# A hybrid encoder layer on one core: the wide input projection from fp32r pairs to scaled fp16 pairs, in two weight passes

## The chip, the core and the metric

The kernel runs on one NeuronCore of a Trainium2 chip. Its engines work through queues of their own: TensorE (PE in the profile, its weight loads PEld), VectorE (DVE), ScalarE (ACT), GpSimd (POOL) and SyncE (SP), whose queue here only issues DMAs. The metric is the device time of one execution in microseconds (us). Of the kernel before there are three timed runs, 911.38, 912.72 and 910.8 us, median 911.38.

## The reference

One layer of a hybrid encoder, 2048 tokens and 16 meta tokens in front of them, width 1024. Tokens are normalised (RMSNorm), and one projection feeds two mixers:

```python
u = rmsnorm(h, norm_g) @ w_in
pool_in, pool_gate, c_q, c_kv, k_r, attn_gate = jnp.split(u, SPLIT_POINTS, axis=-1)   # 512,512,256,128,64,512
pool_out = silu(pool_gate) * pool_mixer(pool_in, pool_w, pool_scale)   # trailing means over 2,4,8,16 tokens
...                                              # low-rank attention, 4 heads, chunks of 64 tokens
attn_out = silu(attn_gate) * attn
h + concat([pool_out, attn_out]) @ w_out         # then a last RMSNorm
```

The change concerns the three parts of the projection that are 512 wide: the pooling input, its gate and the attention gate, 1536 columns together.

## The kernel before

**Split numbers.** To come near fp32, a product is made of three matmuls of pairs: each operand is split into a rounded high part and the remainder, and high*high, low*high and high*low are summed. Scores and projections hold the parts as fp32r. The weighted sum over the values (`pv`, line 470, tiles `o`) has its parts in fp16.

**Stages.** A first stage makes the queries, keys and values of all tokens and starts the attention of the short chunks. The attention follows, chunk by chunk in the order of `ORDER`: chunks 20 to 31 in groups of four, then 19 down to 8. For a chunk `scores` runs twice (two pairs of heads): PE computes score blocks (lines 407 to 411), DVE takes the maximum (line 413), ACT the exponential (line 434), the fp16 pair is made on ACT and on POOL or DVE (lines 437 and 439), and a DMA transpose on SP's queue (line 446) turns it for `pv`. Up to chunk 17 `pv` comes one chunk after its scores, later right behind them.

**The wide projection** is the work of `run_pass` (lines 658 ff.). Its 1536 columns are 12 weight blocks `m` of 128: 0 to 3 the pooling input, 4 to 7 its gate, 8 to 11 the attention gate. The tokens are eight sub-ranges `i`: the first has 272 (16 of them meta), the others 256. `mproj` computes one block on one sub-range as 24 matmuls, 8 slices of the depth by three products. `PASSES = ((0,), (1, 2, 3), (4, 5, 6, 7))` gives three passes over the weights. Within a pass blocks go in pairs (`MORDER`: 0 and 4, 1 and 5, ...), and each pair runs over the pass's sub-ranges. Pass 0 is spread over the attention of the chunks 13 to 8 (`FILL`); passes 1 and 2 follow the attention.

**What is loaded.** `load_w` fetches a block (512 KB) and splits it in four pieces on ACT and on POOL or DVE, once in each pass: 36 times. `load_x` fetches a sub-range in two halves, multiplies by the norm's gain and splits it on ACT and DVE. The token's own factor (`rbc`, one over its root mean square) is applied to the result, line 588 (`u`) and line 611 (`gt`). Sub-range 0 is loaded at chunk 15, sub-ranges 1 to 3 when the attention is over (its memory is used), 4 to 7 in the last pair of pass 1.

**Behind a block**: `pool_in` makes window sums on DVE and splits the result, `gate` makes the SiLU from a tanh, `pool_out` multiplies by the pooling weights (three matmuls, line 620). At the end the output projection (line 800) takes 16 tiles of tokens. Before a tile its operand is split (lines 787 to 790) into the buffers that the weight blocks used.

**Order.** A scheduler puts each engine's instructions in order by times that it simulates. On the chip each engine works through its list in that order, and so does SP with its DMAs.

## Time and profile before

| | us |
|---|---|
| median of three timed runs (910.8 to 912.72) | 911.38 |
| the profiled execution | 913.35 |
| its span, first to last instruction | 911.5 |
| PE busy | 875.0 (96%) |
| DVE, ACT, POOL busy | 569.7, 442.7, 357.4 |
| matmuls of the wide projection, line 579 | 2304 |

The span is what the profiler saw of one execution. A PE matmul's record is longer than the time until the next can start, so that busy time says less than the distance from start to start. PEclk and "granted clock" are the share of TensorE's full clock: 1.0 is 2.4 GHz, 0.5 is 1.2 GHz.

### The profile page before, as it was taken

The page shows a single profiled execution, that of the slowest core. Times are in us where ns is not written, and L with a number is a line of the kernel's source. Part 1 is how long each engine was busy: PE and PEld are TensorE (multiplying, and loading weights), DVE is VectorE, ACT ScalarE, POOL GpSimd, SP SyncE. Part 2 cuts the span into 40 slices and gives each one's busy share as a digit, 9 for nine tenths or more (in the row PEclk, how much of TensorE's full clock was granted, in tenths as well). Part 3 has the DMA queues.
Part 4 walks back from the last instruction along what each step waited for, and adds up shares of the span by engine and source line. Part 5 has one row for each costly group of instructions (what it writes and reads, how often), then busy time and mean ns, then how long its engine had stood idle before and what let it go on. Part 6 is the DMA issues. An engine that isn't in the chain of part 4 may idle for free.

```text
span 911.5 us, 16442 instructions
## 1 busy us (share of the span) xinstructions
PE 875.0 (96%) x5799; PEld 794.2 (87%) x5799; DVE 569.7 (63%) x1309; ACT 442.7 (49%) x1217; POOL 357.4 (39%) x572
## 2 busy tenths in 40 slices
PE   9799899999999999899969999999999999999996
...
PEclk9899999999999999999979999999999999999999
...
GB/s 266 207 175 178 143 48 104 173 142 126 157 154 135 125 161 134 210 177 167 150 209 198 47 93 70 200 90 47 38 34 25 139 93 93 93 92 93 105 81 46
DMA packets 210413, 114.39 MB, mean 125 GB/s; under 512 B 169641, under 2 KB 196747, under 8 KB 210331
## 3 DMA queue, kind: packets, MB, share of 16 engines
...
q8 instruction: 45, 0.74, 0.3%
...
## 4 chain that ended last, share of the span: by engine, by line
PE 69%; DMA 10%; DVE 8%; ACT 6%; issue 4%; POOL 2%; ACTq 0%; SPq 0%; POOLq 0%; DVEq 0%
PE mp L579 26%; PE op L800 20%; PE o L470 6%; PE tok L221 4%; DVE st L413 2%; DMA yr<-hT_in 2%; DMA raw<-hT_in 2%; PE qa L310 2%; ACT p L434 2%; PE s L407 2%; PE s L409 2%; PE s L408 2%; PE s L411 2%; PE s L410 2%; DMA pt<-hl 1%
## 5 line engine op out<-in xcount | busy, mean ns | idle before, releaser
L579 PE MATMUL mp<-y,wh 128*128 128x256 f32 (+1 forms) x1536 | 285.1, 284 | 4.5 <-DVE y L548 2.8
L579 PEld LDWEIGHTS mp<-y,wh 128*128 128x128 f32 x1536 | 242.1, 191 | 5.0 <-DVE y L548 3.0
L579 PE MATMUL mp<-y,wl 128*128 128x256 f32 (+1 forms) x768 | 217.8, 284 | 0.0
L800 PE MATMUL op<-wo,mh 128*128 128x512 f32 (+1 forms) x528 | 160.4, 386 | 0.0
L579 PEld LDWEIGHTS mp<-y,wl 128*128 128x128 f32 x768 | 146.2, 190 | 0.1
L439 POOL TENSOR_TENSOR hl<-p,hl 128x512 f16<-128x512 f32 (+4 forms) x104 | 102.8, 1010 | 98.1 <-ACT hl L437 92.8
L434 ACT ACTIVATE p<-s,st 128x512 f32<-128x512 f32 (+8 forms) x168 | 99.3, 601 | 63.7 <-DVE st L419 51.3
L800 PEld LDWEIGHTS op<-wo,mh 128*128 128x128 f32 x528 | 98.0, 188 | 22.2
L800 PE MATMUL op<-wo,ml 128*128 128x512 f32 (+1 forms) x264 | 102.3, 388 | 0.0
L470 PE MATMUL o<-pt,vh 128*128 128x256 f16 x544 | 92.8, 274 | 6.5 <-DMA pt<-hl 6.2
L413 DVE TENSOR_REDUCE st<-s 128x1 f32<-128x512 f32 (+6 forms) x154 | 88.6, 588 | 15.0 <-PE s L411 14.0
L567 POOL TENSOR_TENSOR wl<-wr,wh 128x256 fp32r<-128x256 f32 x96 | 80.3, 858 | 31.9 <-ACT wh L565 29.5
L437 ACT CAST hl<-p 128x512 f16<-128x512 f32 (+6 forms) x168 | 82.0, 540 | 4.8 <-DMA pt<-hl 4.3
L802 DVE TENSOR_TENSOR xr<-op,xr 128x512 f32<-128x512 f32 (+1 forms) x33 | 22.3, 676 | 92.9 <-PE op L800 92.9
L470 PE MATMUL o<-pt,vl 128*128 128x256 f16 x272 | 74.5, 274 | 0.0
L804 ACT ACTIVATE osq<-xr 128x512 f32<-128x512 f32 (+1 forms) x33 | 20.4, 617 | 97.7 <-DVE xr L802 88.2
L470 PEld LDWEIGHTS <-vh 128*128 128x128 f16 x544 | 51.3, 98 | 17.6 <-issue 5.8
L565 ACT CAST wh<-wr 128x256 fp32r<-128x256 f32 x144 | 47.8, 403 | 31.3 <-PE mp L579 18.1
L789 POOL TENSOR_TENSOR ml<-mix,mh 128x512 fp32r<-128x512 f32 x16 | 21.7, 1355 | 102.0 <-ACT mh L787 102.0
L800 PEld LDWEIGHTS op<-wo,ml 128*128 128x128 f32 x264 | 49.6, 188 | 10.5
L589 POOL COPY carry<-u 128x16 f32<-128x16 f32 x32 | 15.8, 494 | 88.6 <-DVE u L588 88.6
L439 DVE TENSOR_TENSOR hl<-p,hl 128x512 f16<-128x512 f32 (+7 forms) x64 | 42.4, 663 | 12.5 <-ACT hl L437 12.3
...
## 6 DMA issues: line engine op xcount, KB each, us to landing
wr<-w_m_in SPq DMA_DIRECT2D x36, 512.0 KB, 3.7
xt<-hcat_in SPq DMA_DIRECT2D x16, 512.0 KB, 5.0
xr<-hcat_in SPq DMA_DIRECT2D x16, 512.0 KB, 3.7
raw<-hT_in SPq DMA_DIRECT2D x15, 512.0 KB, 6.4
out_dram<-xr SPq DMA_DIRECT2D x15, 512.0 KB, 2.6
yr<-hT_in SPq DMA_DIRECT2D x14, 512.0 KB, 3.8
...
wor<-w_out_in SPq DMA_DIRECT2D x8, 512.0 KB, 4.1
```

The costliest lines, as they stand in the source:

```text
L221: nc.tensor.matmul(ps[:T, :448], lhsT=a[:, k, :T], rhs=w[:, k], start=k + i == 0, stop=k == KT - 1 and i == 2)
L413: nc.vector.reduce_max(out=mx[:, bi:bi + 1], in_=ps[:, :w], axis=AX.X)
L434: nc.scalar.activation(out=pr[:, o:o + w], in_=pss[bi][:, :w], func=AF.Exp, bias=nb_, accum_out=sm[:, bi:bi + 1] if nb > 1 else tot)
L437: nc.scalar.copy(out=hl[:, 0, sl], in_=pr[:, sl])
L439: eng.tensor_tensor(out=hl[:, 1, sl], in0=pr[:, sl], in1=hl[:, 0, sl], op=ALU.subtract)
L470: nc.tensor.matmul(ps[:, :2 * P], lhsT=v, rhs=x, start=i == 0, stop=i == len(ops) - 1)
L565: nc.scalar.copy(out=wh[:, sl], in_=wr[:, sl])
L567: eng.tensor_tensor(out=wl[:, sl], in0=wr[:, sl], in1=f(wh[:, sl]), op=ALU.subtract)
L579: nc.tensor.matmul(ps[:, :n - sk], lhsT=a[:, k], rhs=x[:, k, sk:n], start=e == 0, stop=e == 3 * KT - 1)
L789: nc.gpsimd.tensor_tensor(out=ml[:, 0:4], in0=m, in1=f(mh[:, 0:4]), op=ALU.subtract)
L800: nc.tensor.matmul(ps[:, :w], lhsT=x[:, k], rhs=y[:, sl], start=i == 0, stop=i == 3 * KT - 1)
L802: nc.vector.tensor_add(out=xr[:, sl], in0=ps[:, :w], in1=xr[:, sl])
```

## The change

The two operands of the wide projection become fp16 pairs: high and low parts in fp16 instead of fp32r, three products as before.

- fp16 has a smaller range, so both are multiplied by powers of two first. For the tokens it comes from the largest gain (`gmx`, once, behind the first stage). For a weight block it comes from the block's largest entry: each of the 12 blocks is fetched once more during the attention of the chunks 20 to 31 (`SCAN`, tile `ws`), DVE takes the largest absolute value, and behind the last one `weight_scales` spreads the maxima over the partitions with 12 small fp32 matmuls (one more for `gmx`).
- The token's factor moves into `load_x`: DVE multiplies each slice by gain and `rbc` in place, ACT rounds to fp16, POOL subtracts, in pieces of two slices. The factors at lines 588 and 611 go; what undoes the scales is applied by ACT (`winv`, `whalf`) or within `psi`.
- fp16 tokens need half the memory: `PASSES = ((0, 1), (2, 3, 4, 5, 6, 7))`, 24 block loads for 36. Pass 0 has twice the work in the same places of the attention. Sub-ranges 0 and 1 are loaded at the chunks 17 and 16, 2 and 3 during pass 0, 4 to 7 in the first pair of pass 1.
- `load_w` splits in two pieces of 512: one on ACT and DVE, the other on ACT (twice) and POOL. The output projection's split operands get buffers of their own.

```diff
+WPIECE = 512
+XSC = 9
+WSC = 14
...
+SCAN = {23 - m if m < 4 else 31 - m if m < 8 else 39 - m: m for m in range(12)}
...
+def spread_max(nc, ps, cols, n, ident, out):
+    for i in range(n):
+        nc.tensor.matmul(ps[:, i * P:(i + 1) * P], lhsT=cols[:, i:i + 1].broadcast_to([P, P]), rhs=ident, start=True, stop=True)
+    nc.vector.reduce_max(out=out, in_=ps[:, :n * P].rearrange("p (n q) -> p n q", n=n), axis=AX.X)
...
-    PASSES = ((0,), (1, 2, 3), (4, 5, 6, 7))
+    PASSES = ((0, 1), (2, 3, 4, 5, 6, 7))
...
         for k0 in (0, 4):
-            raw = wtile("wr", 4 * n, F32, f"yr{i}_{k0}", XPOOL.get(i)).rearrange("p (k t) -> p k t", k=4)
+            raw = wtile("wr", 4 * n, F32, f"yr{i}_{k0}").rearrange("p (k t) -> p k t", k=4)
             nc.sync.dma_start(out=raw, in_=hT[:, k0:k0 + 4, o:o + n])
             for k in range(k0, k0 + 4):
-                nc.scalar.mul(out=xh[:, k], in_=raw[:, k - k0], mul=gin_t[:, k:k + 1])
-                nc.vector.scalar_tensor_tensor(out=xl[:, k], in0=raw[:, k - k0], scalar=gin_t[:, k:k + 1], in1=f(xh[:, k]),
-                                               op0=ALU.mult, op1=ALU.subtract)
+                nc.vector.scalar_tensor_tensor(out=raw[:, k - k0], in0=raw[:, k - k0], scalar=gxs[:, k:k + 1], in1=rbc,
+                                               op0=ALU.mult, op1=ALU.mult)
+            for k in (k0, k0 + 2):
+                nc.scalar.copy(out=xh[:, k:k + 2], in_=raw[:, k - k0:k - k0 + 2])
+                nc.gpsimd.tensor_tensor(out=xl[:, k:k + 2], in0=raw[:, k - k0:k - k0 + 2], in1=xh[:, k:k + 2], op=ALU.subtract)
...
+            sc = wsc[:, m:m + 1]
+            for n, o in enumerate(range(0, D, WPIECE)):
+                sl = slice(o, o + WPIECE)
+                if n % 2 == 0:
+                    nc.scalar.mul(out=wh[:, sl], in_=wr[:, sl], mul=sc)
+                    nc.vector.scalar_tensor_tensor(out=wl[:, sl], in0=wr[:, sl], scalar=sc, in1=wh[:, sl], op0=ALU.mult, op1=ALU.subtract)
+                else:
+                    nc.scalar.mul(out=wr[:, sl], in_=wr[:, sl], mul=sc)
+                    nc.scalar.copy(out=wh[:, sl], in_=wr[:, sl])
+                    nc.gpsimd.tensor_tensor(out=wl[:, sl], in0=wr[:, sl], in1=wh[:, sl], op=ALU.subtract)
+            wts[(ps_, m)] = (wh.rearrange("p (k c) -> p k c", k=KT), wl.rearrange("p (k c) -> p k c", k=KT))
...
-        nc.vector.tensor_tensor(out=u[:, 16:16 + n], in0=ps[:, :n], in1=rbcs[i], op=ALU.mult)
+        nc.scalar.mul(out=u[:, 16:16 + n], in_=ps[:, :n], mul=winv[:, g:g + 1])
...
-        nc.vector.tensor_tensor(out=gt, in0=ps[:, :G], in1=rbcs[i][:, n - G:n], op=ALU.mult)
-        nc.scalar.activation(out=th, in_=gt, func=AF.Tanh, scale=0.5)
-        nc.vector.scalar_tensor_tensor(out=gt, in0=th, scalar=1.0, in1=gt, op0=ALU.add, op1=ALU.mult)
+        nc.scalar.activation(out=th, in_=ps[:, :G], func=AF.Tanh, scale=whalf[:, m:m + 1])
+        if m < 8:
+            nc.vector.scalar_tensor_tensor(out=gt, in0=th, scalar=1.0, in1=ps[:, :G], op0=ALU.add, op1=ALU.mult)
+        else:
...
+                if ps_ == 0 and pi == 2 * XPRE[n]:
+                    load_x(2 + n)
+                if ps_ == 0 and pi == len(MORDER) - 2 and n == 0:
+                    load_w(1, *MORDER[0:2])
+                if ps_ == 1:
+                    if pi == 0 and n < 4:
...
+        if c in SCAN:
+            m = SCAN[c]
+            ws = att2.tile([P, D], F32, name=f"ws{m}", tag="ws", bufs=2)
+            with tc.issue_after(last_tr[0]):
+                nc.sync.dma_start(out=ws, in_=w_m[m])
+            nc.vector.tensor_reduce(out=wmx[:, m:m + 1], in_=ws, axis=AX.X, op=ALU.max, apply_absolute_value=True)
+            if m == 11:
+                weight_scales()
...
+        if c == X1_AT:
+            load_x(1)
+        if c == W0_AT:
+            load_w(0, *MORDER[0:2])
...
-        mh = wtile("wh", D, F32R, f"mh{t}").rearrange("p (k t) -> p k t", k=KT)
-        ml = wtile("wl", D, F32R, f"ml{t}").rearrange("p (k t) -> p k t", k=KT)
+        mh = c2.tile([P, D], F32R, name=f"mh{t}", tag="mh", bufs=2).rearrange("p (k t) -> p k t", k=KT)
+        ml = c2.tile([P, D], F32R, name=f"ml{t}", tag="ml", bufs=2).rearrange("p (k t) -> p k t", k=KT)
```

What moved, by the order of the instructions (a name holds its block or chunk, then a buffer number: `pt23_0` is the first transposed page of chunk 23, `mp1_4` block 4 on sub-range 1, `yr4_0` the raw tokens of sub-range 4, `x2` the fp16 tokens of the sub-ranges 4 and 5).

SP's queue at the change from chunk 7 to chunk 23, before:

```order
L446 DMA_TRANSPOSE pt7_1_1944<-hl7_0_1_1937 128x5x128
L446 DMA_TRANSPOSE pt7_0_1934<-hl7_1_0_1965 128x4x128
L446 DMA_TRANSPOSE pt7_1_1944<-hl7_1_1_1971 128x5x128
L446 DMA_TRANSPOSE pt23_0_2064<-hl23_0_0_2060 128x8x128
L446 DMA_TRANSPOSE pt23_1_2071<-hl23_0_1_2067 128x8x128
```

And in the change:

```order
L472 DMA_TRANSPOSE pt7_1_1961<-hl7_0_1_1954 128x5x128
L472 DMA_TRANSPOSE pt7_0_1951<-hl7_1_0_1982 128x4x128
L472 DMA_TRANSPOSE pt7_1_1961<-hl7_1_1_1988 128x5x128
L798 DMA ws0_2044<-w_m_in 128x1024
L472 DMA_TRANSPOSE pt23_0_2084<-hl23_0_0_2080 128x8x128
L472 DMA_TRANSPOSE pt23_1_2091<-hl23_0_1_2087 128x8x128
```

The fetch of a block's scan now stands between the transposes of two chunks, and so it does for twelve chunks.

PE's queue behind the last attention product (`av2`), before:

```order
L494 MATMUL av2_1_6293<-ol2_5800,wvh_121 128x256
L494 MATMUL av2_1_6293<-oh2_5799,wvh_121 128x256
L494 MATMUL av2_1_6293<-oh2_5799,wvl_122 128x256
L494 MATMUL av2_1_6293<-ol2_5800,wvh_121 128x256
L579 MATMUL mp1_0_6427<-y1_6404,wh1_0_6365 128x256
L579 MATMUL mp1_0_6427<-y1_6404,wl1_0_6366 128x256
L579 MATMUL mp1_4_6464<-y1_6404,wh1_4_6377 128x256
L579 MATMUL mp1_4_6464<-y1_6404,wl1_4_6378 128x256
```

In the change, the same place and the place where the sub-ranges 4 and 5 (`x2`) are first used:

```order
L520 MATMUL av2_1_6756<-oh2_6136,wvl_129 128x256
L520 MATMUL av2_1_6756<-ol2_6137,wvh_128 128x256
L611 LDWEIGHTS wh1_4_6837
L611 MATMUL mp2_4_6961<-x1_5644,wh1_4_6837 128x256
L611 LDWEIGHTS wh1_0_6830
```

```order
L611 MATMUL mp3_4_7050<-x1_5644,wh1_4_6837 128x256
L654 MATMUL pm2_0_7079<-plh2_0_6957,pwh_4835 128x256
L654 MATMUL pm2_0_7079<-plh2_0_6957,pwl_4836 128x256
L654 MATMUL pm2_0_7079<-pll2_0_6958,pwh_4835 128x256
L611 LDWEIGHTS wh1_0_6830
L611 MATMUL mp4_0_7106<-x2_6990,wh1_0_6830 128x256
L611 LDWEIGHTS wl1_0_6831
L611 MATMUL mp4_0_7106<-x2_6990,wl1_0_6831 128x256
```

Before, PE meets a sub-range that is fetched after the attention (`y1`) at once. Now 99 matmuls of `mp1_11`, `mp2_0`, `mp2_4`, `mp3_0` and `mp3_4` stand between the last `o` matmul and the first on `x2`; the fp16 matmuls have weight loads of their own.

POOL's queue there, before:

```order
L684 TENSOR_TENSOR at0_1536<-at0_1536,gt0_10_6326 128x256
L567 TENSOR_TENSOR wl1_4_6378<-wr1_4_6375,wh1_4_6377 128x256
L684 TENSOR_TENSOR at0_1536<-at0_1536,gt0_11_6356 128x256
L567 TENSOR_TENSOR wl1_4_6378<-wr1_4_6375,wh1_4_6377 128x256
L567 TENSOR_TENSOR wl1_1_6520<-wr1_1_6517,wh1_1_6519 128x256
L589 COPY carry_5082<-u1_0_6452 128x16
L567 TENSOR_TENSOR wl1_1_6520<-wr1_1_6517,wh1_1_6519 128x256
L587 COPY u2_0_6566<-carry_5082 128x16
```

In the change:

```order
L621 COPY carry_4806<-u2_0_6949 128x16
L619 COPY u3_0_7038<-carry_4806 128x16
L725 TENSOR_TENSOR at1_2021<-at1_2021,gt1_11_6899 128x256
L578 TENSOR_TENSOR x2_6990<-yr4_4_7003,x2_6990 128x512 x2
L844 TENSOR_TENSOR ml0_9663<-mix0_4808,mh0_9662 128x512
L844 TENSOR_TENSOR ml1_9733<-mix0_4808,mh1_9732 128x512
L578 TENSOR_TENSOR x2_6990<-yr5_0_7086,x2_6990 128x512 x2
L621 COPY carry_4806<-u3_0_7038 128x16
L578 TENSOR_TENSOR x2_6990<-yr4_0_6993,x2_6990 128x512 x2
L578 TENSOR_TENSOR x2_6990<-yr5_4_7096,x2_6990 128x512
L619 COPY u4_0_7131<-carry_4806 128x16
L578 TENSOR_TENSOR x2_6990<-yr5_4_7096,x2_6990 128x512
```

The subtractions of the tokens are now POOL's, and two of the output projection's operands (`ml0`, `ml1`) have come forward between them. Before they stand behind the whole of the wide projection.

## Rows read from the trace of the kernel before

**Rows 1.** The page's slices: busy tenths in 40 slices, granted clock.

```profile
PE   9799899999999999899969999999999999999996
...
PEclk9899999999999999999979999999999999999999
```

**Rows 2.** Busy time by stretch; columns in the second line.

```profile
core 0: us, PE busy (x) PEld busy (x) DVE busy (x) ACT busy (x) POOL busy (x), PEclk, DMA share, GB/s
180.00:360.00 180.00, 178.82 (x1226) 157.86 (x1225) 117.46 (x288) 123.12 (x352) 82.29 (x108) 1.00 0.84 142
360.00:440.00 80.00, 76.54 (x569) 71.18 (x567) 65.89 (x155) 53.42 (x157) 43.89 (x69) 1.00 0.79 182
440.00:460.00 20.00, 16.50 (x136) 15.71 (x134) 15.64 (x44) 13.47 (x46) 12.14 (x19) 1.00 0.57 138
460.00:480.00 20.00, 13.89 (x84) 12.38 (x85) 8.72 (x20) 7.61 (x20) 2.57 (x4) 0.74 0.83 241
480.00:490.00 10.00, 9.18 (x74) 8.80 (x74) 10.00 (x25) 7.84 (x22) 5.89 (x8) 1.00 0.60 183
490.00:720.00 230.00, 230.00 (x1922) 230.00 (x1921) 158.63 (x346) 75.38 (x197) 85.51 (x131) 1.00 0.26 80
```

**Rows 3.** The chain that ended last, in order of time: start us, us, what.

```profile
41.59 3.75 PE we L284 x16
...
301.86 5.25 PE o L470 x48
...
463.01 7.31 DMA yr<-hT_in
...
686.08 40.24 PE mp L579 x336
726.32 178.09 PE op L800 x792
```

**Rows 4.** Line 579: duration ns min/median/max, first and last start us, forms.

```profile
L579 PE MATMUL mp<-y,wh x1536: 274/283/582, 383.2 to 726.0; 128*128 128x256 f32 x184, 128*128 128x272 f32 x8
...
L579 PE MATMUL mp<-y,wl x768: 274/283/415, 383.4 to 725.9; 128*128 128x256 f32 x184, 128*128 128x272 f32 x8
```

**Rows 5.** PE in time, the instructions after idle time: start, us, what [idle <-releaser].

```profile
460.49 0.38 PE L470 MATMUL o<-pt,vh 128*128 128x256 f16 x2 [2.44 <-DMA pt<-hl]
...
468.25 0.39 PE L579 MATMUL mp<-y,wh 128*128 128x256 f32 x1 [1.70 <-ACT y L547]
...
471.81 0.80 PE L579 MATMUL mp<-y,wh 128*128 128x256 f32 x2 [2.83 <-DVE y L548]
```

**Rows 6.** Groups on POOL by form: xcount | busy us, mean ns | idle before.

```profile
L439 POOL TENSOR_TENSOR hl<-p,hl 128x512 f16<-128x512 f32 x36 | 45.3, 1261 | 69.6 <-ACT hl L437 67.9 <-issue 1.1 <-DVE ql L314 0.5
...
L789 POOL TENSOR_TENSOR ml<-mix,mh 128x512 fp32r<-128x512 f32 x16 | 21.7, 1355 | 102.0 <-ACT mh L787 102.0
L589 POOL COPY carry<-u 128x16 f32<-128x16 f32 x32 | 15.8, 494 | 88.6 <-DVE u L588 88.6
...
L587 POOL COPY u<-carry 128x16 f32<-128x16 f32 x32 | 11.2, 351 | 8.4 <-DVE pl L599 6.2 <-issue 1.1
```

**Rows 7.** A group on DVE by form.

```profile
L653 DVE TENSOR_TENSOR wo<-wor,wo 128x1024 fp32r<-128x1024 f32 x8 | 9.6, 1246 | 1.9 <-ACT wo L652 1.8
```

**Rows 8.** DVE in time, from 483 us.

```profile
484.30 1.66 DVE L548 SCALAR_TENSOR_TENSOR y<-yr,gains_t,y 128x256 fp32r<-128x256 f32 x4
...
486.55 0.41 DVE L604 TENSOR_TENSOR pll<-pl,plh 128x256 fp32r<-128x256 f32 x1
...
487.91 0.41 DVE L599 SCALAR_TENSOR_TENSOR pl<-w,u 128x256 f32<-128x256 f32 x1
```

**Rows 9.** POOL in time, from 483 us.

```profile
486.43 1.95 POOL L589 COPY carry<-u 128x16 f32<-128x16 f32 x1 [2.66 <-DVE u L588]
```

**Rows 10.** DMA issues: xcount, KB each, median us from issue to landing.

```profile
wr<-w_m_in SPq DMA_DIRECT2D x36, 512.0 KB, 3.7
...
pt<-hl SPq DMA_TRANSPOSE x168, 3.2
```

More of the change, by code (lines that the diff above doesn't have):

```diff
@@ L11 @@
 F16 = mybir.dt.float16
+I32 = mybir.dt.int32
 AF = mybir.ActivationFunctionType
@@ L50 @@
 WRB = 2
-XPOOL = {1: 0, 2: 1, 3: 0}
 TBB = 2
@@ L121, in hymba @@
     nc.gpsimd.memset(rall, 1.0)
+    gxs = cp.tile([P, KT], F32, name="gxs")
+    ginv = cp.tile([P, 1], F32, name="ginv")
+    wsc = cp.tile([P, 12], F32, name="wsc")
+    winv = cp.tile([P, 12], F32, name="winv")
+    whalf = cp.tile([P, 12], F32, name="whalf")
+    psi = cp.tile([P, H], F32, name="psi")
+    wmx = cp.tile([P, 12], F32, name="wmx")
     ca_cm, cap = open_pool("ca", side="left")
@@ L345, in hymba @@
     pts = {}
+    last_tr = [None]
     rsum = {}
@@ L542, in load_x @@
-        xl = l_[:, :KT * n].rearrange("p (k t) -> p k t", k=KT)
+        if i // 2 not in xpairs:
+            xpairs[i // 2] = big((1, 0, 2, 3)[i // 2], f"x{i // 2}", F16, 2 * KT * (SUBS[i][1] + SUBS[i + 1][1]))
+        at = 0 if i % 2 == 0 else 2 * KT * SUBS[i - 1][1]
+        xp = xpairs[i // 2][:, at:at + 2 * KT * n].rearrange("p (a k t) -> p a k t", a=2, k=KT)
+        xh, xl = xp[:, 0], xp[:, 1]
+        rbc = cw["pool"].tile([P, n], F32, name=f"rbc{i}", tag="rbc", bufs=2, padded_shape=[P, 272])
@@ L620, in pool_out, with weight_scales @@
             nc.tensor.matmul(ps[:, :G], lhsT=w[:, g], rhs=x, start=e == 0, stop=e == 2)
-        nc.vector.scalar_tensor_tensor(out=mixg[i][:, g], in0=ps[:, :G], scalar=psh_t[:, g:g + 1],
+        nc.vector.scalar_tensor_tensor(out=mixg[i][:, g], in0=ps[:, :G], scalar=psi[:, g:g + 1],
                                        in1=gt, op0=ALU.mult, op1=ALU.mult)
     cw = {}
+    def weight_scales():
+        for m in range(0, 12, 4):
+            spread_max(nc, bank("m", f"wmx{m}"), wmx[:, m:m + 4], 4, ident, wsc[:, m:m + 4])
+        power_scale(nc, wsc, winv, wsc, WSC)
+        nc.vector.tensor_scalar(out=winv, in0=winv, scalar1=ginv, scalar2=float(2.0 ** -WSC), op0=ALU.mult, op1=ALU.mult)
+        nc.vector.tensor_scalar(out=whalf, in0=winv, scalar1=0.5, scalar2=None, op0=ALU.mult)
+        nc.vector.tensor_tensor(out=psi, in0=psh_t, in1=winv[:, 4:8], op=ALU.mult)
     def pre_c(pool):
@@ L630, in pre_c @@
         nc.gpsimd.memset(cw["carry"], 0.0)
-        mixg[0] = pool.tile([P, H, G], F32, name="mix0")
+        for i in PASSES[0]:
+            mixg[i] = pool.tile([P, H, G], F32, name=f"mix{i}")
         load_x(0)
-        load_w(0, MORDER[0])
-        load_w(0, MORDER[1])
         pw_r = wtile("wr", H * P, F32, "pw_r")
```

128 lines of the change are left out of this document (59 added, 69 removed).

## The prediction

> **What bounds the kernel now.** I read the page's slices first: PE is busy 90% or more in nearly all of them, and the clock falls in one slice in the middle [rows 1]. Busy PE time is no proof of a bound, so I cut the run into stretches [rows 2]. From 490 to 720 us, where only the wide projection runs, PE is busy 230.00 of 230 us while DVE has 159, POOL 86 and DMA a quarter: there the time is the number of matmuls by the distance between their starts. In the attention (180 to 360 us) PE is idle 1.2 us of 180, with DVE and ACT at two thirds, POOL under a half and DMA at 0.84. The one stretch in which PE waits is the handover, 440 to 490 us: idle 3.50, 6.11 and 0.82 us, in sum 10.4, and in its middle part the granted clock is 0.74 of full speed. PE's instructions in time name the waits [rows 5]: 2.44 us for the last transposed page, 1.70 and 2.83 us for the tokens that are fetched when the attention is over; the chain has their DMA with 7.31 us there [rows 3].
>
> **The change part by part.**
>
> *A, the matmuls.* 1536 and 768, together 2304 matmuls [rows 4]; 96 have 272 columns and are priced like the rest. The chain has 336 of them, without a break, in 40.24 us: 119.8 ns from start to start [rows 3]. An fp16 matmul of as many columns, with another weight load before each, stands in the same kernel: 48 of line 470 in 5.25 us, 109.4 ns [rows 3]. 2304 x 10.4 ns = 24.0 us less. None of it lies beside other work where PE is the bound. 1728 of the 2304 stand in the second pass, where nothing else binds; if the 576 in the attention bring nothing, 18.0. I take 24.0.
>
> *B, the handover.* Before, it costs 10.4 us of idle time and some clock: a mean of 0.74 over 20 us means 10.4 us at half speed; PE works in 13.89 of the 20, so about 7.2 us of its work took twice as long, 3.6 us. Together 14.0 us [rows 2]. In the change PE has more to do there: the order shows 99 matmuls ahead of the first on sub-range 4, and 144 more ahead of sub-range 7. From 460.5 us, where the last `o` begins [rows 5], PE has 15 of those (1.6 us), 12 for `av` and 12 for `pm` (2.8 at 0.12) and 243 x 0.1094 = 26.6: it wants sub-range 7 at 491.5 us. What is late next is POOL. The first of these tokens land at 463.01 + 7.31 = 470.3 us [rows 3]. Then POOL has 16 subtractions of 512 at 1.261 us, two output operands of 1.355 that the order has brought forward, two halves of weight blocks (1.261 each) and some eleven copies of 0.35 to 0.49 [rows 6]: 20.2 + 2.7 + 2.5 + 4.6 = 30.0, so it ends at 500.3, and PE waits 8.8 us. Ends: if the tokens come as fast as their fetch, no wait, 14.0 us gained. If DVE's two-input work and POOL's never overlap, DVE's 32 token instructions (0.415 each by four in 1.66 us [rows 8]), 18 steps of the window sums at 0.41 and two weight halves at 0.62 lie on top, 13.3 + 7.4 + 1.2 = 21.9, and PE waits 31: 17 us lost. I take 9 us of waiting, 5.0 us gained.
>
> *C, the scans.* Twelve times 512 KB and a maximum over 1024 columns on DVE. The nearest row, a subtraction of 1024 columns, takes 1.246 us [rows 7]: 15.0 us of DVE, from 117 to 132 of its 180. The DMA, 6.3 MB beside 142 GB/s x 180 us = 25.6 MB, would lift the share of 0.84 to about 0.98 at the 241 GB/s of the handover [rows 2]. A fetch takes 3.7 us to land, a transpose 3.2 [rows 10], and the order puts each fetch in front of a chunk's transposes on SP's queue. `pv` comes one chunk later, which hides a few us. Behind each maximum on DVE wait the sums that start a chunk's exponentials. Ends: 0 and 15.0 (all of DVE's part in the open). PE's idle time of 1.2 us speaks for the low end: 3.5 us.
>
> *D, the scales.* 13 fp32 matmuls of 128 columns; 16 of that form took 3.75 us [rows 3]: 3.0 us on PE, which is the bound there. The small DVE steps behind them wait for nobody's work but their own. Ends: 0, if they fall into PE's waits, and 6.0 at half the clock.
>
> *E, twice the work in pass 0.* Between 360 and 440 us PE is idle 3.5 of 80 us, DVE busy 66 of 80 [rows 2]. PE's additional matmuls are moved from a later place, so they are no cost by themselves. DVE gets three more sub-ranges of tokens (24 x 0.415 = 10 us) and one more of windows and gates (30 instructions of about 0.41, 12 us), while PE's 288 more matmuls at 109 ns make the stretch longer by 31 us: DVE's share stays near 0.8. Ends: -3.5 (all idle time gone) and +8 (two chunks' exponentials late). I take +1.
>
> The 12 block loads that go, and the factors that move from DVE to ACT behind a block, lie beside a PE that is busy all the time: nothing. The output projection (792 in 178.09 us [rows 3]) stays.
>
> **Sum.** -24.0 - 5.0 + 3.5 + 3.0 + 1.0 = -21.5 us. From the profiled execution's 913.35 that is 891.9. It is 2.0 above the median of the timed runs; taken from 911.38 it is 889.9. I say 890.
>
> **The rivals.**
>
> *1, DVE and POOL shut each other out.* At 486.43 us a copy of 16 columns on POOL, 0.35 to 0.49 us as a rule, took 1.95 us, while DVE went from 486.55 to past 487.91 without a pause through two-input work [rows 6, 8, 9]. The tokens of sub-ranges 4 to 7 now need both engines, in turns. Against it: POOL's 1.261 us is a mean over the attention, where DVE is busy two thirds of the time [rows 2, 6], so that it holds a share of such waits already. If half of the 21.9 us comes on top in the handover, and the clock falls once more there, B is a loss of 8 instead of a gain of 5, and the time 903. Chance 0.13. The Trainium skill (SBUF — State Buffer, section Who interferes with whom) states it as a rule: a VectorE instruction with two SBUF inputs and a GpSimd instruction that reads SBUF share a port pair by an exclusive lock, and the second waits for the whole of the first. The copy of 1.95 us agrees.
>
> *2, the scans hold up the transposes; slower.* For it: DMA at 0.84 already, one queue for both. Against it: in 180 us PE waited 1.2 us [rows 2], so the transposes have room. Its price is at most 1.25 + 3.7 us for each of 12, 59 us. It decides once more than 25.0 us of that (-24.0 - 5.0 + 3.0 + 1.0) lie open, 2.1 us in each chunk. Half of it open: 25.0 against 29.7, 916 us. Chance 0.04.
>
> *3, the distance between starts stays 120 ns,* because something other than the number format sets it in these loops. For it: in the loops of the projection nothing but fp32r was ever run. Against it: the 109.4 ns. Then A is 0 and the rest +2.5: 914. Chance 0.03.
>
> *4, all is covered:* the handover's waits vanish, scans and pass 0 cost nothing: -24.0 - 14.0 + 3.0 - 3.5, 873; half way there, 881. Chance 0.12.
>
> **How the numbers follow.** My forecast, 883 to 900, has 0.68. The range of 8 in 10 takes in most of rivals 1 and 4: 879 to 903. A measurement of this kernel can tell 0.2%, 1.8 us, from no change. Faster by more: 0.68 + 0.13 + 0.12 = 0.93. Rivals 2 and 3 leave 0.02 for within and 0.05 for slower.
>
> **What the profile afterwards would show.** A: 48 matmuls of the projection in 5.25 us, and some 2304 x 109 ns in all. B: PE's waits behind the last `av`, released by POOL's token subtractions, of about 9 us before block 0 of sub-range 7 is through, and the copy or `ml0` in front of them on POOL. C: PE idle in the attention under 5 us, few waits for pages. D: `wmx` and `gmx`, 3 us. E: little idle time between the chunks 15 and 10. I am wrong if the projection's matmuls keep 120 ns, if the waits for pages in the attention exceed 10 us, or if the handover costs more than it did.

## Result and profile after

The changed kernel takes 920.91 us (median of 4 runs, 920.72 to 921.78), the kernel before 912.04 beside it (4 runs, 910.8 to 912.72). The ratio is 1.0101, 95% interval 1.0083 to 1.0118: slower by about 1%. The forecast was 890, faster. The profiled execution has a span of 920.0 us against 911.5, at a mean granted clock of 0.986 against 0.988.

The page's slices of the changed kernel (40 slices, tenths of a slice), to be laid beside [rows 1]:

```profile
PE   9799899898998999789999978999999999999996
PEclk9899999999999999899999989999999999999999
```

There are more 8s and 7s than before, and two dips of the clock instead of one. Cut into stretches (columns as in [rows 2]):

```profile
180.00:360.00 180.00, 170.65 (x1145) 148.73 (x1143) 125.34 (x292) 114.62 (x323) 80.21 (x101) 1.00 0.88 163
360.00:440.00 80.00, 67.94 (x524) 58.90 (x524) 56.79 (x124) 49.03 (x126) 38.53 (x48) 0.96 0.73 164
440.00:520.00 80.00, 74.86 (x613) 66.07 (x612) 57.33 (x134) 51.05 (x131) 34.94 (x49) 1.00 0.55 127
520.00:580.00 60.00, 50.21 (x407) 42.32 (x406) 48.92 (x79) 30.94 (x60) 36.31 (x38) 0.91 0.53 159
580.00:720.00 140.00, 139.45 (x1270) 124.79 (x1269) 70.50 (x150) 50.45 (x108) 34.77 (x56) 1.00 0.14 42
```

PE now waits 9.35 us in the attention (1.2 before), 12 of 80 us in the next stretch, and 9.8 of 60 in the handover, which has moved from 440-490 to 520-580. Only behind 580 us is it busy all the time. The chain of waits (start, us, what):

```profile
285.23 4.65 DMA ws<-w_m_in
372.57 5.91 DMA rbc<-rd
525.32 3.71 DMA yr<-hT_in
530.38 4.19 DVE yr L574 x3
542.39 3.90 DVE yr L574 x4
575.25 5.26 PE mp L611 x48
677.09 57.66 PE mp L611 x528
```

48 matmuls in 5.26 us are 109.6 ns each, 528 in 57.66 are 109.2: the rate that was forecast. The rest is new to the chain [rows 3]: scans, token factors, tokens.

To see where the time goes I compare starts of the same instruction. Three stretches: I, from the 168th of the 840 score matmuls (behind the first of the twelve scans) to the 620th (PE's work in it is that of the kernel before plus the scales' 12 matmuls, 24 passes, in every other kernel); II, from there to the 839th, the end of the attention; III, from there to the first matmul of the output projection (`op`). Differences of starts in the one profiled execution of each kernel, in us; times are medians, and a kernel's profiled execution may lie a few us from its median: e1's lies 4.9 above, e9's 4.3 above, e7's 3.8 below. In the nine kernels that leave stretch I alone (the changed one, e6, e7, e9, e11, e14, e15, e16, e18) it lies between 179.2 and 182.1, so a difference of up to 3 us between two rows says nothing.

| kernel | time | ratio to before (95%) | I | II | III |
|---|---|---|---|---|---|
| before | 912.0 | | 163.7 | 116.0 | 278.4 |
| changed | 920.9 | 1.0101 (1.0083 to 1.0118) | 179.5 | 160.2 | 227.7 |
| e1 no scans | 915.6 | 1.0045 (1.0019 to 1.0070) | 170.2 | 167.6 | 229.8 |
| e2 short maximum | 930.2 | 1.0213 (1.0190 to 1.0236) | 184.7 | 168.0 | 226.2 |
| e3 maximum alone | 916.8 | 1.0065 (1.0041 to 1.0088) | 169.3 | 161.4 | 225.7 |
| e4 maximum late | 934.7 | 1.0255 (1.0225 to 1.0284) | 180.2 | 173.2 | 227.1 |
| e5 maximum behind sums | 928.1 | 1.0195 (1.0176 to 1.0213) | 175.0 | 174.4 | 228.2 |
| e6 tokens behind ri | 924.7 | 1.0163 (1.0137 to 1.0189) | 180.5 | 165.1 | 227.4 |
| e7 no POOL tokens | 915.4 | 1.0058 (1.0036 to 1.0080) | 180.0 | 161.0 | 218.1 |
| e8 = e5 + e6 | 931.4 | 1.0226 (1.0194 to 1.0258) | 173.8 | 172.4 | 228.9 |
| e9 no tokens 0, 1 | 914.4 | 1.0046 (1.0025 to 1.0066) | 179.4 | 157.5 | 228.5 |
| e10 = e1 + e7 + e9 | 896.1 | 0.9826 (0.9784 to 0.9869) | 170.1 | 155.9 | 218.6 |
| e11 two blocks first | 923.4 | 1.0142 (1.0107 to 1.0178) | 179.7 | 162.9 | 229.5 |
| e12 candidate | 926.2 | 1.0169 (1.0137 to 1.0201) | 174.7 | 168.5 | 229.3 |
| e13 = e5 + e9 | 912.9 | 1.0012 (0.9987 to 1.0037) | 175.7 | 156.4 | 226.4 |
| e14 low parts on DVE | 921.3 | 1.0107 (1.0062 to 1.0152) | 179.2 | 162.0 | 226.5 |
| e15 one in pass 0 | 924.5 | 1.0124 (1.0090 to 1.0158) | 180.7 | 131.4 | 258.4 |
| e16 = e14 + e15 | 923.1 | 1.0111 (1.0075 to 1.0146) | 182.1 | 131.9 | 258.4 |
| e17 factors behind blocks | 916.5 | 1.0055 (1.0034 to 1.0076) | | | |
| e18 the same for 2 to 7 | 913.2 | 1.0017 (0.9992 to 1.0043) | 181.0 | 165.4 | 213.1 |

(e17's profiled execution was a slow one, 925.1 us, and its stretches are left out. The kernel before was timed again beside each group of runs, at medians of 910.2 to 912.0; the ratios go by these.)

The account of the change, by the forecast's terms: 2304 matmuls at 119.8 - 109.6 = 10.2 ns give -23.5 (A). Stretch I is 15.8 longer (C and D). Stretch II is 44.2 longer; 29.9 of that is work moved into it (240 `mp` at 109.6, 16 `o` at 109.4, 15 `pm` at some 120 ns), and its own 240 `mp` save 2.4, so 16.7 is lost (E). Stretch III should be shorter by 50.9 (240 `mp` moved out at 119.8 = 28.8, 1824 at 10.2 ns = 18.6, 16 `o` and 15 `pm` = 3.6) and is by 50.7: the handover neither gains nor loses, 0.2 (B). Ahead of stretch I 1.0 is gained. -23.5 + 15.8 + 16.7 + 0.2 - 1.0 = 8.2 of the 8.5 us between the spans.

**Stretch I.** What VectorE's maximum waits for (idle time of the engine before it, in us and times):

```profile
L799 DVE TENSOR_REDUCE wmx<-ws x12: 1219/1220/1222, 158.3 to 319.8; 128x1 f32<-128x1024 f32 x12
its engine sat idle before it (us, times) until:
  DMA ws<-w_m_in: 24.3, 12
DMA to landing us min/median/max: 4.0/4.7/6.1
```

Twelve maxima of 1.22 us work 14.6 us, but VectorE stands 24.3 us more in front of them, 2.0 for each, because the fetch sits behind the last chunk's transposes on SP's queue and takes 4.7 us to land. PE feels it one step later, by scores that wait for exponentials, 1.0 us in the kernel before (PE's waits, 180 to 360 us: us in total, times, longest):

```profile
PE s L433 <- ACT p L460: 7.8, 8, 1.5
```

**Stretch II.** PE's waits from 360 to 520 us, and VectorE at the first of them:

```profile
PE rt L380 <- DVE ri L378: 9.1, 2, 6.8
PE s L433 <- ACT p L460: 3.4, 3, 2.7
PE o L496 <- DMA pt<-hl: 2.3, 3, 1.5
```
```profile
378.09 1.82 DVE L574 SCALAR_TENSOR_TENSOR yr<-yr,gxs,rbc 128x272 f32<-128x272 f32 x4 [2.35 <-DMA yr<-hT_in]
...
381.52 2.69 DVE L574 SCALAR_TENSOR_TENSOR yr<-yr,gxs,rbc 128x272 f32<-128x272 f32 x4
...
384.66 0.19 DVE L378 RECIPROCAL ri<-rs 128x8 f32<-128x8 f32 x1
```

The reciprocal of group 4, for whose transpose PE waits 6.8 us, stands behind both halves of the tokens of sub-range 0, with 2.35 us of waiting for their fetch. The granted clock is 0.83 between 380 and 400 us.

**Stretch III.** PE's longest waits from 520 to 580 us, and what VectorE and GpSimd do then:

```profile
PE mp L611 <- ACT x L577: 6.9, 3, 5.4
PE pm L654 <- ACT plh L635: 2.1, 1, 2.1
```
```profile
522.91 1.67 DVE L574 SCALAR_TENSOR_TENSOR yr<-yr,gxs,rbc 128x256 f32<-128x256 f32 x4 [2.66 <-DMA yr<-hT_in]
...
529.49 5.08 DVE L574 SCALAR_TENSOR_TENSOR yr<-yr,gxs,rbc 128x256 f32<-128x256 f32 x4 [1.69 <-POOL x L578]
...
542.31 3.97 DVE L574 SCALAR_TENSOR_TENSOR yr<-yr,gxs,rbc 128x256 f32<-128x256 f32 x4
```
```profile
530.14 2.86 POOL L844 TENSOR_TENSOR ml<-mix,mh 128x512 fp32r<-128x512 f32 x2
532.97 1.33 POOL L578 TENSOR_TENSOR x<-yr,x 128x512 f16<-128x512 f32 x1
...
543.30 2.69 POOL L578 TENSOR_TENSOR x<-yr,x 128x512 f16<-128x512 f32 x2
```

The same four products take 1.67 us beside a GpSimd that only makes two short copies, and 5.08 or 3.97 while it subtracts; the 5.08 lie mostly beside two operands of the output projection (`ml`) that the order brought forward. PE's longest wait, 5.4 us, is for a high part that ACT rounds behind such products. All 32 of the four sub-ranges (busy us, mean ns), and two other groups of VectorE from 517 to 566 us:

```profile
L574 DVE SCALAR_TENSOR_TENSOR yr<-yr,gxs,rbc 128x256 f32<-128x256 f32 x32 | 23.2, 783 | 4.3 <-DMA yr<-hT_in 2.7 <-POOL x L578 1.7
L631 DVE SCALAR_TENSOR_TENSOR pl<-w,u 128x256 f32<-128x256 f32 x5 | 4.6, 924 | 0.1
L644 DVE SCALAR_TENSOR_TENSOR gt<-th,mp 128x256 f32<-128x256 f32 x5 | 2.0, 405 | 0.0
```

Line 631 reads two operands from SBUF and is held up too; line 644, of the same size, has one of its two (`mp`) in PSUM and is not.

### The profile page after: what moved, and what is told of

The parts are those of the page before. It is cut to its first block, busy times and chain, and to the rows that moved or that the text cites. A ratio compares the mean times of both kernels' runs of the same rounds, so it can differ in the third digit from the quotient of the medians.

```text
span 920.0 us, 16228 instructions
## 1 busy us (share of the span) xinstructions
PE 860.7 (94%) x5825; PEld 745.6 (81%) x5825; DVE 550.3 (60%) x1217; ACT 459.6 (50%) x1177; POOL 348.6 (38%) x532
## 4 chain that ended last, share of the span: by engine, by line
PE 57%; DVE 14%; DMA 12%; ACT 6%; issue 5%; POOL 3%; SPq 2%; ACTq 0%; POOLq 0%; DVEq 0%
PE mp L611 20%; PE op L855 19%; PE tok L246 5%; PE o L496 4%; DVE yr L574 3%; DVE st L439 3%; DMA ws<-w_m_in 2%; PE tok L215 2%; ACT p L460 2%; DMA pt<-hl 2%; DMA yr<-hT_in 2%; SPq L472 2%; POOL hl L465 2%; DVE hl L465 1%; ACT hl L463 1%
## 5 line engine op out<-in xcount | busy, mean ns | idle before, releaser
L611 PE MATMUL mp<-x,wh 128*128 128x256 f16 (+1 forms) x1536 | 262.9, 275 | 7.0 <-ACT x L577 6.9
L611 PE MATMUL mp<-x,wl 128*128 128x256 f16 (+1 forms) x768 | 211.3, 276 | 0.2 <-DVE wl L595 0.2
L611 PEld LDWEIGHTS <-wh 128*128 128x128 f16 x1536 | 150.8, 99 | 20.5 <-issue 0.2
L465 POOL TENSOR_TENSOR hl<-p,hl 128x512 f16<-128x512 f32 (+4 forms) x104 | 104.8, 1028 | 120.7 <-ACT hl L463 118.9
L611 PEld LDWEIGHTS <-wl 128*128 128x128 f16 x768 | 75.8, 99 | 17.2 <-issue 7.4
L855 PEld LDWEIGHTS op<-wo,ml 128*128 128x128 f32 x264 | 49.6, 188 | 10.8
L642 ACT ACTIVATE th<-mp,whalf 128x256 f32<-128x256 f32 x64 | 30.1, 471 | 51.8 <-PE mp L611 49.4
L465 DVE TENSOR_TENSOR hl<-p,hl 128x512 f16<-128x512 f32 (+7 forms) x64 | 44.2, 690 | 12.3 <-ACT hl L463 9.7
L433 PE MATMUL s<-klo,qh 128*128 128x512 f32 (+9 forms) x116 | 44.5, 384 | 5.0 <-ACT p L460 5.0
L578 POOL TENSOR_TENSOR x<-yr,x 128x512 f16<-128x512 f32 (+1 forms) x32 | 41.4, 1308 | 15.5 <-ACT x L577 15.4
```

What stands on the lines that cost most here:

```text
L433: nc.tensor.matmul(ps[:, :w], lhsT=q(qh), rhs=kt[:, 0, 0, sl], start=True, stop=False)
L465: eng.tensor_tensor(out=hl[:, 1, sl], in0=pr[:, sl], in1=hl[:, 0, sl], op=ALU.subtract)
L578: nc.gpsimd.tensor_tensor(out=xl[:, k:k + 2], in0=raw[:, k - k0:k - k0 + 2], in1=xh[:, k:k + 2], op=ALU.subtract)
L611: nc.tensor.matmul(ps[:, :n - sk], lhsT=a[:, k], rhs=x[:, k, sk:n], start=e == 0, stop=e == 3 * KT - 1)
L642: nc.scalar.activation(out=th, in_=ps[:, :G], func=AF.Tanh, scale=whalf[:, m:m + 1])
L855: nc.tensor.matmul(ps[:, :w], lhsT=x[:, k], rhs=y[:, sl], start=i == 0, stop=i == 3 * KT - 1)
```

## The experiments

All start from the changed kernel; I, II and III are the table's.

**e1, no scans.** Fetch and maximum out, `wmx` set to a constant.
```diff
-                nc.sync.dma_start(out=ws, in_=w_m[m])
-            nc.vector.tensor_reduce(out=wmx[:, m:m + 1], in_=ws, ...)
+    nc.gpsimd.memset(wmx, 0.125)
```


> Leaves the scans out: the twelve maxima are set to 0.125 at the start instead of being read from the weights, so the twelve fetches of 512 KB and the twelve maxima on VectorE are gone; the 12 small fp32 matmuls and everything behind them stay. The trace of the changed kernel shows PE about 15 us later at 325 us than before, with the score matmuls waiting for exponentials. If the scans cause that, by whichever of their parts: about 906 us. If the 15 us come from something else in the attention (the four fp32r chunks that are unchanged, the query preparation), no change: 921.

915.6. I falls by 9.3 to 170.2, and PE's share of the attention is that of the kernel before (178.82 [rows 2]):

```profile
180.00:360.00 180.00, 178.86 (x1232) 157.90 (x1231) 117.61 (x289) 119.17 (x339) 80.97 (x104) 1.00 0.78 140
```

The scans cost 9 us there; the time falls by 5.3 only, so some 4 are lost again behind it (II is 7.4 longer, in an execution 4.9 above the median). Of the 15.8 in I, 6.5 are left without the scans, the scales (D) among them.

**e2, short maximum; e3, maximum alone.**
```diff
 e2
-... in_=ws, axis=AX.X, ...
+... in_=ws[:, 0:16], axis=AX.X, ...
 e3
-                nc.sync.dma_start(out=ws, in_=w_m[m])
-... in_=ws, axis=AX.X, ...
+... in_=f(klo[:, 0, 0, 0:D]), axis=AX.X, ...
```


> The fetches stay whole, the maximum runs over 16 of the 1024 columns (the scale then comes from a part of the weights). VectorE still stands in its queue until each fetch has landed (24.3 us of waiting in the changed kernel) but works some 0.1 us instead of 1.22. If the wait in VectorE's queue is what costs: 24.3 of 24.3 + 14.6 us stay, so about 10 of the 15 us stay, 916. If the work of the maximum is what costs: 906. If it is the 6.3 MB on the DMA engines that delay the transposed pages: 921.

> The maximum is taken, at full length, over 1024 columns of keys that lie in SBUF, and the fetches are left out (the scales then come from the keys, not from the weights). VectorE's 14.6 us of work stay, its 24.3 us of waiting and the DMA's 6.3 MB go. If the wait costs: 909 to 911 (5 of 15 us stay). If the work costs: 921. If the DMA engines' load costs: 906.

930.2 and 916.8. Without the work but with fetch and wait, I is no shorter (184.7); with the work but without fetch and wait it is as in e1 (169.3). VectorE's 14.6 us of maxima cost nothing by themselves. Why e2 is 5 us longer than the changed kernel in I isn't settled.

**e4, maximum late; e5, maximum behind sums.**
```diff
 e4, at the next chunk's start
+        for m, ws in late:
+            nc.vector.tensor_reduce(out=wmx[:, m:m + 1], in_=ws, ...)
 e5, after the next chunk's first half
+                with tc.issue_after(last_sum[0]):
+                    nc.vector.tensor_reduce(out=wmx[:, m:m + 1], in_=ws, ...)
```


> Nothing is left out: each fetch is issued where it was, its maximum is taken one chunk later (some 8 us), when it has landed. VectorE's work and the DMA's bytes stay, the wait of 24.3 us goes. If the wait costs: 910 to 912. If the work or the bytes cost: 921.

> Nothing is left out. In the kernel with the maximum one chunk later the order on VectorE had stayed as it was, and VectorE waited 23.8 us for the fetches. Here each maximum is tied behind the sum of the exponentials of the next chunk's first half, about half a chunk later, so it stands on VectorE where its fetch should long have landed; work and bytes stay. By the way this order also puts the reciprocal of the fifth group (ri of group 4) ahead of the tokens of sub-range 0. If VectorE's wait is what the scans cost: the maximum waits under 3 us in all, PE is about 10 us earlier at 325 us, and 904 to 911. If the bytes on the DMA engines or the 14.6 us of work cost: as the changed kernel in the attention, 914 to 921.

934.7 and 928.1. e4 is a miss of the edit: the order on VectorE left the maxima where they were, and they waited 25.4 us. I is as in the changed kernel; why II is 13.0 longer isn't settled. In e5 the same view shows no wait:

```profile
L807 DVE TENSOR_REDUCE wmx<-ws x12: 1208/1209/1212, 165.4 to 323.3; 128x1 f32<-128x1024 f32 x12
its engine sat idle before it (us, times) until:
who waited for it (us, times):
  POOL hl L458: 0.7, 1
```

I is 175.0, as it is in e8, e12 and e13 (173.8 to 175.7) with the same edit: the wait cost 4 to 6 us. Another 4 to 6 go only in e1, e3 and e10, which leave the fetches out; whether these are the 6.3 MB or the maxima's new place isn't told apart, for in e5 PE's longest waits from 180 to 360 us are for other results of VectorE (`cl` 2.7, `ol` 2.6 us). But II grew by 14 and the time by 7. In the order on VectorE the first weight block now stands 15 places later, and PE's first `mp` starts 65.2 us behind the 620th score matmul instead of 59.7.

**e6, tokens behind ri; e8, both.**
```diff
-C1_AT = 17
-X1_AT = 16
-W0_AT = 15
+C1_AT = 16
+X1_AT = 15
+W0_AT = 14
+            with tc.issue_after(last_ri[0]):
+                pre_c(c1)
```


> The tokens of sub-range 0, then those of 1 and the first weight blocks, are asked for one chunk later, and VectorE's part of sub-range 0 is tied behind the reciprocal (ri) of group 4, for whose transpose PE waited 7.0 us at 385 us in the changed kernel. The scans stay. If the gap comes from the tokens that stand ahead of this reciprocal: the gap goes, about 914. If PE then waits as long for the first weight block or the same tokens, only later: 921.

> Both edits in one kernel: the maxima behind the sums, and the tokens one chunk later behind the reciprocal. Nothing is left out. If each of the two waits costs by itself: 921 - 10 - 7 = 904, faster than the kernel before (911). If a wait that is taken away in the attention comes back at the handover: 915 or more.

924.7 and 931.4. The wait of 6.8 us for `ri` went in e6, and II became 4.9 us longer all the same: 3.1 us of waiting for exponentials, 3.3 for the query preparation and 1.1 for the first block stood in its place between 375 and 412 us.

**e7, no POOL tokens; e14, low parts on DVE.**
```diff
 e7 (i >= 4)
-                nc.gpsimd.tensor_tensor(out=xl[:, k:k + 2], ..., op=ALU.subtract)
+                nc.scalar.copy(out=xl[:, k:k + 2], in_=raw[:, k - k0:k - k0 + 2])
 e14 (i >= 4)
+                nc.vector.tensor_tensor(out=xl[:, k:k + 2], ..., op=ALU.subtract)
```


> Leaves out the subtraction that makes the low parts of the tokens of sub-ranges 4 to 7: a copy on ScalarE fills them instead of GpSimd's subtraction (the low parts are then wrong). In the changed kernel the 32 token products of these sub-ranges took 23.2 us on VectorE, those in groups of four between 1.66 us with GpSimd quiet and 5.08 us beside its subtractions. If the two engines shut each other out: each group of four in about 1.7 us, 13.4 us in all, the handover from 520 to 580 us loses some 6 us less of PE, 913 to 916. If the tokens' fetch sets the pace, or ScalarE, which makes the high parts: 921.

> Nothing is left out: the low parts of the tokens of sub-ranges 4 to 7 are subtracted on VectorE instead of GpSimd, 16 instructions of some 0.75 us, 12 us more on VectorE; its 32 products should take 13.4 us instead of 23.2 as no subtraction of GpSimd stands beside them. If the two engines shut each other out, the sum on VectorE hardly grows and GpSimd's part is for nothing: 915 to 917. If they really work side by side, VectorE is now late by the 12 us: 925 to 930.

915.4 and 921.3. III falls by 9.6 in e7 (in an execution 3.8 below its median) and by 1.2 in e14. VectorE's token instructions from 515 us on, e7 and then e14 with its subtractions:

```profile
L574 DVE SCALAR_TENSOR_TENSOR yr<-yr,gxs,rbc 128x256 f32<-128x256 f32 x32 | 17.2, 591 | 6.4 <-DMA yr<-hT_in 5.7 <-DMA rbc<-rd 0.7
```
```profile
L574 DVE SCALAR_TENSOR_TENSOR yr<-yr,gxs,rbc 128x256 f32<-128x256 f32 x32 | 15.9, 554 | 4.8 <-DMA yr<-hT_in 2.4 <-POOL wl L600 2.4
L579 DVE TENSOR_TENSOR x<-yr,x 128x512 f16<-128x512 f32 x16 | 11.4, 735 | 0.0
L632 DVE SCALAR_TENSOR_TENSOR pl<-w,u 128x256 f32<-128x256 f32 x5 | 2.1, 419 | 0.0
```

e14's VectorE does the products and GpSimd's part in 27.3 us, against 23.2 for the products alone, and PE is no later: the 11.4 us of subtractions came to 4.1 more on these rows, and VectorE's other two-input work, no longer held up, pays a part of that back (line 632, which was line 631: 2.1 us for 4.6). The time fell between the two expectations.

**e9, no tokens 0 and 1; e10, three out.**
```diff
 def load_x(i):
+        if i < 2:
+            xs[i] = (vh, vl)
+            return
```


> Leaves out the preparation of the tokens of sub-ranges 0 and 1: the projection of these two reads fp16 values of the attention (vh, vl) instead, so 4 fetches of 0.5 MB, 16 products on VectorE, 8 copies on ScalarE and 8 subtractions on GpSimd are gone between 370 and 400 us; PE's matmuls stay. In the changed kernel PE loses 13.7 us between 360 and 420 us, the kernel before 5.3. If the tokens cause it: 912 or 913. If PE would wait there for the first weight block or the next chunk's exponentials anyway, or loses it later: 919 to 921.

> Leaves out three things at once: the scans (constant maxima), the preparation of the tokens of sub-ranges 0 and 1, and GpSimd's subtraction for those of 4 to 7 (a copy on ScalarE). If these three are all that eats the gain of the faster matmuls, and they add up: 921 - 11 (the scans, as PE's lateness in the attention shows it) - 8 - 8 = 894, near the forecast of 890. If a gain upstream is lost again further down, as in the kernels so far: 905 or more.

914.4 and 896.1. Together the three take 24.8 us off the time, where each by itself took 5.3, 5.5 and 6.5 (by the ratios 25, and 5.1, 3.9 and 5.0). In e10 stretch III is 218.6 and I 170.1, as with each edit alone: there the gains add up. II is 4.3 us shorter than in the changed kernel and 11.7 shorter than in e1: the tokens of 0 and 1 seem to cost more when the scans are gone. PE's waits in II are others now (336 to 493 us; then VectorE at the second of them):

```profile
PE o L497 <- DMA pt<-hl: 4.8, 6, 1.1
PE pm L661 <- DVE st L445: 4.8, 1, 4.8
```
```profile
446.07 1.67 DVE L578 SCALAR_TENSOR_TENSOR yr<-yr,gxs,rbc 128x256 f32<-128x256 f32 x4 [3.12 <-DMA yr<-hT_in]
...
449.16 2.26 DVE L578 SCALAR_TENSOR_TENSOR yr<-yr,gxs,rbc 128x256 f32<-128x256 f32 x4
```

These are tokens of the sub-ranges 2 or 3, as 0 and 1 are left out. VectorE stands 3.12 us for their fetch, and the step that PE waits for until 452.07 us stands behind them. e9 and e13 have the same single wait of 4.8 us.

**e13, late maxima and no tokens.** e5's and e9's edits.

> The maxima behind the sums, and in addition the preparation of the tokens of sub-ranges 0 and 1 left out (the projection reads vh and vl for them). With the maxima behind the sums alone PE was 15 us earlier than in the changed kernel at 361 us, and 6 us later at 510. If the tokens are where that was lost: the whole gain stays, 902 to 906. If it was lost because the order of everything behind had changed, or to the two chunks' own work: 915 or more.

912.9, between the two. II is 156.4, 18.0 shorter than in e5: with the tokens of 0 and 1 gone, what e5 lost there is gone too. I is 3.8 shorter than in the changed kernel, II and III are 1.1 and 2.1 shorter than in e9; where the rest of the expected gain went isn't told apart.

**e11, two blocks first; e12, candidate.** e12 is e11 with e5's edit and `W0_AT = 16`, `X1_AT = 15`.
```diff
+        if ps_ == 1:
+            k = len(subs)
+            cols = cols[0:2] + cols[k:k + 2] + cols[2:k] + cols[k + 2:]
...
+                if at == 0:
+                    load_w(1, *MORDER[2:4])
```


> Nothing is left out. At the start of the second pass PE runs the first two pairs of weight blocks over sub-ranges 2 and 3, which are ready, before it turns to 4 to 7: 10.5 us more of matmuls stand ahead of the tokens that it waits for. The second pair of blocks is prepared that much earlier. If the handover costs because VectorE and GpSimd are late with the tokens: PE loses some 8 us less between 520 and 580 us, 911 to 914. If the second pair's preparation makes both engines later by as much: 919 to 922.

> Nothing is left out. The second pass as in the kernel with two pairs of blocks first, the maxima behind the sums, and the first weight blocks asked for ahead of the tokens of sub-range 1. If the gains of the attention and the handover both stay: 921 - 8 - 8 = 905. If the attention's gain is lost again between 360 and 510 us, as it was with the maxima behind the sums alone: 915 to 920.

923.4 and 926.2. III is no shorter (229.5): 10.5 us more of PE's work in front did not help. The second pair of blocks is prepared by the same two engines: from 540 to 560 us VectorE works 19.96 of 20 us, and between 505 and 580 us PE now waits 4.1 us for a block's low part on VectorE.

**e15, one in pass 0; e16, with e14's edit.**
```diff
-    PASSES = ((0, 1), (2, 3, 4, 5, 6, 7))
+    PASSES = ((0,), (1, 2, 3, 4, 5, 6, 7))
-    WOSLOT = (1, 4, 0, 2)
+    WOSLOT = (4, 1, 0, 2)
+                if ps_ == 0 and pi in (2, 4, 6):
+                    load_x(pi // 2)
```


> Nothing is left out, two passes stay: sub-range 0 alone in the first, 1 to 7 in the second, as many matmuls and weight blocks in all, 288 matmuls moved out of the attention; the tokens of 1 to 3 are prepared one after the other beside the first pass. If preparing two sub-ranges between 370 and 400 us costs 8 us more than one, and the handover waits because only two sub-ranges are ready: 906 to 912. If VectorE and GpSimd set the pace of the handover however much is ready, and the first tokens alone cost the same: 918 to 922.

> Nothing is left out: sub-range 0 alone in the first pass, and the low parts of 4 to 7 on VectorE. If both help by themselves and add up: 902 to 907. If they are two ways to the same 8 us of the handover: as the better of them, 908 to 914.

924.5 and 923.1. II now holds the same matmuls as in the kernel before, 10.2 ns faster each, and is still 15.4 us longer; PE waits 6.9 us for the same `ri`. So the doubled first pass is not the cause of E. What e15 still shares with the changed kernel is that the tokens of four sub-ranges are prepared there. III is 258.4, where the matmuls alone would give 257.3, so its handover gains nothing either. e16 is 1.3 us faster than e15, within both intervals: the low parts on VectorE bring nothing here.

**e17 and e18, factors behind blocks.**
```diff
+                    nc.scalar.mul(out=xh[:, k], in_=raw[:, k - k0], mul=gxs[:, k:k + 1])
+                    nc.vector.scalar_tensor_tensor(out=xl[:, k], in0=raw[:, k - k0], scalar=gxs[:, k:k + 1],
+                                                   in1=xh[:, k], op0=ALU.mult, op1=ALU.subtract)
...
+            nc.vector.scalar_tensor_tensor(out=gt, in0=ps[:, :G], scalar=winv[:, m:m + 1], in1=rbcs[i][:, n - G:n], ...)
```


> Nothing is left out. For sub-ranges 0, 1 and 4 to 7 the tokens' own factor (rbc) is applied behind a block, on VectorE, as in the kernel before; ahead of it ScalarE makes the scaled high part and VectorE the low part in one product-and-difference each, so VectorE keeps 8 instructions a sub-range and GpSimd's 24 subtractions, with the wait for rbc, go. fp16 pairs, scans and two passes stay. VectorE gets 72 instructions of some 0.42 us more behind blocks, 24 of them in the attention. If the exclusion of GpSimd and VectorE is what the tokens cost, at both places: 5 us from the handover, as without GpSimd's tokens, and 3 to 5 in the attention: 911 to 913. If VectorE's amount of work sets the attention's pace: its 10 us more there come on top, 918 to 922.

> Nothing is left out. The same edit for sub-ranges 2 to 7 alone: the attention's first pass works as in the changed kernel, the second pass has 72 factors more behind blocks on VectorE, which is busy half of the time there. If the exclusion at the handover costs what the kernel without GpSimd's tokens gained (5.5 us): 914 to 916. If VectorE's amount of work sets the handover, since the blocks' factors come on top of the same 32 token instructions: 919 to 924.

916.5 and 913.2. In e18 III is 213.1, 14.6 shorter than in the changed kernel, and PE hardly waits in the handover:

```profile
520.00:580.00 60.00, 59.05 (x533) 52.30 (x531) 51.00 (x109) 37.89 (x83) 21.89 (x30) 1.00 0.63 194
```
```profile
L583 DVE SCALAR_TENSOR_TENSOR x<-yr,gxs,x 128x256 f16<-128x256 f32 x32 | 14.9, 517 | 0.4 <-ACT x L582 0.4
```

VectorE has as many token instructions, and even more work in all (51.0 us for 48.9); GpSimd has 14 us less. So VectorE's amount of work does not set the handover. But the edit does two things: it ends the subtractions beside VectorE, and it makes the high part on ACT straight from the fetch, no longer behind VectorE's product. What each is worth isn't told apart; e7, which ends the subtractions alone, has 9.6 of the 14.6. And 5.2 of the 14.6 are lost in II (165.4 for 160.2). e18 is 7.7 us faster than the changed kernel and, at 1.0017 (0.9992 to 1.0043), the same as the kernel before. e17, with the edit at sub-ranges 0 and 1 too but not at 2 and 3, gains 4.4 on the changed kernel; it is 3.3 slower than e18 by the medians, the intervals overlap, and where it would lose stays open. No kernel here that computes everything beats the kernel before.

## Why the prediction was wrong

The terms missed by 0.5 us (A), 5.2 (B), 9.3 (C and D) and 15.7 (E).

**A was right:** -24.0 forecast, -23.5 measured. The matmuls take 109.6 ns from start to start, so rival 3 is out.

**C and D failed in the price of the wait: 6.5 forecast, 15.8 measured.** The step said that PE's idle time of 1.2 us spoke for the low end, and priced the maxima by VectorE's work. The work is free (e3). What costs is that the maximum stands in VectorE's queue in front of other work until its fetch has landed, 24.3 us of standing still, of which 4 to 6 us reach PE (e5). Another 4 to 6 go with the fetches (e1 and e3 against e5), by their bytes or by the maxima's new place in e5. The bound on the fetch, 3.7 us to land, was in the working [rows 10], but laid upon the transposes and not upon the engine that waits. Rival 2 had the right sign and a wrong mechanism: PE waits for no page between 180 and 360 us. D is within the 6.5 that e1 leaves: 2.8 for the matmuls (24 passes of line 80), some 2 at 170 us, where PE waits for `cl` in this kernel (2.3) and in e1 (2.2) and waited 0.4 before; the rest isn't told apart. That the forecast's 3.0 fits is luck: the 16 of the row that it took as matmuls are passes, two for each of 8 matmuls, and they ran at a mean granted clock of 0.52 (41 to 46 us), so it had half as many passes at twice the time of one (0.112 us here).

**E failed most: +1 forecast, with ends of -3.5 and 8; 16.7 measured.** The step said that a VectorE busy 0.8 of the stretch has room for 24 tokens and 30 windows. VectorE is busy less than that (56.79 of 80) and PE waits all the same: what stands in front of a reciprocal, a maximum or a sum on VectorE can be paid by PE at once. The wait of 6.8 us for `ri` shows it, and e15 that it isn't the doubled pass. That it bites here because `pv` has no chunk's lag any more is argued, not tried. The tokens of 0 and 1 take 2.7 us of it by themselves (e9, no more than two executions may differ), 11.7 with the scans out (e1 to e10), 18.0 when the maxima come late (e5 to e13). Some 13 us of II remain with these tokens out (155.9 to 157.5 against 116.0 + 29.9 - 2.4 = 143.5). The tokens of 2 and 3, which the kernel before prepared after the attention, are work that is new there: one wait of 4.8 us in e9, e10 and e13 stands behind them and their fetch. Leaving them out was not tried. The loss changes its place with each edit, and the scheduler moves other instructions with it, so the cause is settled only in part.

**B: -5.0 forecast, nothing measured (0.2 lost), by rival 1's mechanism.** The forecast set 9 us of waiting for GpSimd's last subtraction against the 14.0 of the handover before. PE does wait 9.8 us between 520 and 580, but mostly for high parts on ACT (6.9), behind products of VectorE that GpSimd's subtractions hold up: four in 1.67 or in 5.08 us, all 32 in 23.2 us where the forecast had 13.3. That the waiting has the forecast's size is luck. What the step put at nothing is the clock: a mean of 0.91 over these 60 us is, by the prediction's own working, 10.8 us at half speed with PE at work 50 of 60, some 4.5 us. 9.8 + 4.5 = 14.3, as much as before. Without the subtractions on GpSimd III is 9.6 shorter (e7), with the shorter way of e18 14.6. The Trainium skill (SBUF — State Buffer, Who interferes with whom) gives this rule for VectorE instructions with two SBUF inputs; the trace agrees, 783 ns a product against 517 for e18's, also with two inputs. I gave rival 1 0.13 as a loss of 13 us on the forecast; the mechanism came, at 5 us.

Rival 4, all covered (873, half way 881), was reached by no run; e10, with three things left out, comes to 896.1.
